# Block loads moved from the SP queue to GpSimd's queue with a cast, in a matmul with rotary embedding on one Trainium2 core

## Chip, core and metric

The kernel runs on one core of one Trainium2 chip. The metric is device time in microseconds (us) of a whole execution. A profile gives the span between the first and the last instruction; in the profiled runs the time is 1.8 us more than the span (161.65 and 159.9 before). The profiled run of before is not one of the four timed ones below. "Slow" is a run that takes over 1.5% more than the fastest of the same kernel in the same call, "fast" any other; the ratios use fast runs alone, while a median quoted is that of all runs unless said.

## The reference

```python
# x (16, 512, 768), weight (768, 768), cos and sin (512, 64), 12 heads of 64
y = np.matmul(x, weight).reshape(batch, seq, n_heads, head_dim)
y1, y2 = y[..., :32], y[..., 32:]
out1 = y1 * cos1 - y2 * sin1
out2 = y2 * cos2 + y1 * sin2
return np.concatenate([out1, out2], axis=-1).reshape(batch, seq, hidden)   # fp32
```

## The kernel before

The rows are worked through in 64 tiles of 128 rows, two tiles to a pair, 32 pairs. A tile has to be cast to FP16 and transposed before TensorE can multiply it. Most tiles ("plain") are cast by ScalarE, transposed by TensorE into PSUM and copied out by ScalarE. Every third pair from pair 8 on (8, 11, ... 29, "block pairs") spares TensorE the transposes: VectorE transposes 32 x 32 blocks. For that a block pair is loaded in four quarters, each to 32 partitions.

```python
BLOCKS = range(8, NP, 3)                 # NP = 32 pairs
xpool = ctx.enter_context(tc.tile_pool(name="xpool", bufs=8))    # plain tiles, fp32
bpool = ctx.enter_context(tc.tile_pool(name="bpool", bufs=3))    # block pairs, fp32
...
def load_quarter(n, q):
    ...
    src = x[b : b + 2].rearrange("b (j a r) (q k) -> r q a (b j) k", r=SB, a=R, q=NQ)
    dst = xbs[n].rearrange("p s (j k) -> p (s j) k", j=NQ)
    nc.sync.dma_start(out=dst[ts(q, R)], in_=src[r, q])     # 32 partitions, 256 rows of 768 bytes

def load_pair(n):
    if n >= NP or n in BLOCKS:
        return
    for s in (0, 1):
        load(n, s)                                          # 128 partitions, rows of 3072 bytes
        for m in (n + 1, n + 2):
            if m in BLOCKS:
                load_quarter(m, (0, 2, 1, 3)[2 * (n + 2 - m) + s])
...
def transpose_blocks(n, s):
    xT = tpool.tile([P, NT, P, 2], FP16, tag="xT", name="xT")
    nc.vector.transpose(out=xT.bitcast(FP32).rearrange("p t m e -> p (t m e)"),
                        in_=x16.pop((n, s)).bitcast(FP32))
...
def rope_pair(n, step=2 * H):
    ps = psys[n].rearrange("p b n -> p (b n)")
    for c in range(0, 2 * H, step):
        rope(n, c, c + step, ps[:, ds(c, step)])            # VectorE: PSUM times cos and sin
        add(n, c, c + step, nc.gpsimd)                      # GpSimd: the sum, into the output tile
...
for n in range(2, NP):
    load_pair(n + AHEAD - 2)                                # AHEAD = 7
    for s in (0, 1):
        for c in CHUNKS:
            mm(n, s, *c)
        upto("turn", 2 * n + s + 3)                         # transposes ahead
        upto("cast", 2 * n + s + 5)                         # casts ahead, ScalarE
    ...
    if n >= 3:
        store(n - 3, nc.scalar)
    rope_pair(n, H if n == NP - ALONE - 1 else 2 * H)       # ALONE = 4
```

## Time and profile before

| | before |
|---|---|
| time, four runs | 163.4, 163.8, 164.32 and (slow) 166.51 us; median 164.06, of the fast ones 163.8 |
| span of the profiled run | 159.9 us |
| TensorE / VectorE / ScalarE / GpSimd busy | 93 / 77 / 55 / 69% |
| bytes moved, mean rate | 53.13 MB, 332 GB/s |

### The profile page before, as it was taken

The numbers are of one execution on the slowest core, as the hardware profiler recorded it, in microseconds if no ns is written. First come the engines' busy times: TensorE is split into PE (matmuls) and PEld (weight loads), VectorE is DVE, ScalarE is ACT, GpSimd is POOL, SyncE is SP. The second block draws the span as 40 slices with busy tenths as digits, with TensorE's granted clock in tenths as the row PEclk, the third lists the DMA queues.
The fourth block names the chain that finished last, engine by engine and source line by source line (L and its number), as shares of the span: only waits on it lengthen the run. The fifth ranks groups of instructions, "written<-read, shape, count | busy, mean of one in ns | idle before, by whom it ended". The sixth has DMA issues, their size and how long they took to land.

```text
span 159.9 us, 2729 instructions
## 1 busy us (share of the span) xinstructions
PE 148.0 (93%) x1074; PEld 93.5 (58%) x1074; DVE 123.1 (77%) x77; ACT 87.6 (55%) x109; POOL 110.9 (69%) x43
## 2 busy tenths in 40 slices
PE   7999999999999999999999999299999999999920
PEld 2455666666666666666666666166667666665610
DVE  0566966788697697697889696459696898699990
ACT  3431966776827746674875854494956697200000
POOL 1000397777888878878878887735868778999990
PEclk9999999999999999999999999999999999999995
DMA  5999999999999999999999999999999999699655
GB/s 172 329 413 395 403 326 267 294 328 370 386 407 268 297 406 364 221 350 414 285 322 404 294 410 398 295 309 376 262 353 388 342 415 373 231 394 377 246 214 197
DMA packets 25837, 53.13 MB, mean 332 GB/s; under 512 B 2016, under 2 KB 10720, under 8 KB 25824
## 3 DMA queue, kind: packets, MB, share of 16 engines
q1 hardware_dynamic: 17056, 28.06, 57.2%
q10 hardware_dynamic: 8768, 24.91, 39.6%
q8 instruction: 8, 0.13, 0.3%
q14 instruction: 5, 0.04, 0.1%
HBM read 27.79 MB, written 25.17 MB: 331 GB/s over the span
## 4 chain that ended last, share of the span: by engine, by line
PE 65%; DMA 23%; DVE 5%; POOL 2%; ACT 2%; issue 1%; POOLq 0%; ACTq 0%; DVEq 0%
PE psy L169 52%; DMA xb<-in_x_dram 10%; PE pt L128 7%; DMA xs<-in_x_dram 7%; DMA out_dram<-ov 7%; DVE tq L183 3%; PE psy L253 3%; PE psz L169 2%; POOL ov L194 2%; ACT xT L72 1%; DVE xT L74 1%; ACT xc L72 1%; DVE xc L74 1%; POOLq L392 0%; ACTq L243 0%
## 5 line engine op out<-in xcount | busy, mean ns | idle before, releaser
L194 POOL TENSOR_TENSOR ov<-tq 128x1536 f32<-128x1536 f32 (+2 forms) x37 | 110.2, 2988 | 44.7 <-DVE tq L183 44.7
L169 PE MATMUL psy<-w_sb,xT 128*128 128x256 f16 (+1 forms) x733 | 126.5, 326 | 0.4 <-DVE w_sb L112 0.2
L183 DVE TENSOR_TENSOR tq<-psy,csn 128x3072 f32<-128x3072 f32 (+3 forms) x39 | 102.9, 2658 | 21.4 <-PE psy L169 20.0
L169 PEld LDWEIGHTS <-xT 128*128 128x128 f16 x769 | 73.4, 98 | 45.3 <-issue 0.6
L72 ACT COPY xT<-pt 128x768 f16<-128x768 f16 x46 | 36.4, 799 | 31.5 <-PE pt L128 31.5
L72 ACT CAST xc<-xs 128x768 f16<-128x768 f32 x46 | 40.8, 904 | 17.8 <-DMA xs<-in_x_dram 17.7
L128 PE MATMUL pt<-ident,xc 128*128 128x128 f16 x288 | 23.9, 221 | 3.4 <-ACT xT L72 3.1
L128 PEld LDWEIGHTS <-xc 128*128 128x128 f16 x288 | 20.0, 99 | 10.3 <-ACT xc L72 3.1
L72 ACT CAST xc<-xb 128x768 f16<-128x768 f32 x16 | 14.3, 903 | 0.5 <-issue 0.4
L135 DVE STREAM_TRANSPOSE xT<-xc 128x384 f32<-128x384 f32 x16 | 8.5, 557 | 3.2 <-ACT xc L72 3.2
L253 PE MATMUL psy<-cold 128*128 128x512 f16 x17 | 6.5, 528 | 1.2 <-DVE cold L260 1.2
L169 PE MATMUL psz<-w_sb,xT 128*128 128x512 f16 (+1 forms) x36 | 6.3, 326 | 0.0
L112 DVE CAST w_sb<-w_raw 128x768 f16<-128x768 f32 (+2 forms) x7 | 3.4, 501 | 2.0 <-DMA w_raw<-in_weight_dram 2.0
L183 DVE TENSOR_TENSOR tq<-psz,csn 128x512 f32<-128x512 f32 (+1 forms) x5 | 4.3, 897 | 0.1
L74 DVE CAST xc<-xs 128x768 f16<-128x768 f32 x2 | 1.9, 948 | 2.9 <-DMA xs<-in_x_dram 2.9
L253 PEld LDWEIGHTS <-cold 128*128 128x128 f16 x17 | 2.0, 128 | 3.5 <-issue 2.2
L74 DVE COPY xT<-pt 128x768 f16<-128x768 f16 x2 | 1.1, 558 | 1.9 <-PE pt L128 1.9
L72 ACT ACT_TABLE_LOAD x1 | 1.3, 1283 | 0.7 <-PEq L378 0.7
L260 DVE MEMSET cold<- 128x256 uint32 x1 | 0.3, 272 | 0.9 <-PEq L378 0.9
L226 DVE TENSOR_TENSOR ov<-psz,tq 128x512 f32<-128x512 f32 x1 | 0.7, 692 | 0.0
L222 DVE TENSOR_TENSOR psz<-psz,csn 128x512 f32<-128x512 f32 x1 | 0.7, 690 | 0.0
L222 DVE TENSOR_TENSOR tq<-psz,csn 128x512 f32<-128x512 f32 x1 | 0.7, 681 | 0.0
(8 smaller groups left out, 1.4 us busy)
## 6 DMA issues: line engine op xcount, KB each, us to landing
out_dram<-ov ACTq DMA_DIRECT2D x28, 768.0 KB, 8.0
xs<-in_x_dram SPq DMA_DIRECT2D x48, 384.0 KB, 8.1
xb<-in_x_dram SPq DMA_DIRECT2D x32, 192.0 KB, 8.7
out_dram<-ov ACTq DMA_DIRECT2D x7, 384.0 KB, 2.4
w_raw<-in_weight_dram SPq DMA_DIRECT2D x5, 384.0 KB, 6.9
w_raw<-in_weight_dram SPq DMA_DIRECT2D x1, 256.0 KB, 5.6
out_dram<-ov SPq DMA_DIRECT2D x1, 256.0 KB, 2.9
w_raw<-in_weight_dram SPq DMA_DIRECT2D x1, 128.0 KB, 5.5
```

The costliest lines, as they stand in the source:

```text
L72: eng.copy(out=o, in_=i_)
L74: eng.tensor_copy(out=o, in_=i_)
L112: nc.vector.tensor_copy(out=w_sb[:, t, e, c0:c1], in_=w_raw[:, t, e, c0:c1])
L128: nc.tensor.transpose(pt[:, t, e, :], xc[:, t, e, :], ident)
L135: nc.vector.transpose(out=xT.bitcast(FP32).rearrange("p t m e -> p (t m e)"), in_=x16.pop((n, s)).bitcast(FP32),)
L169: nc.tensor.matmul(ps[:, a - lo : z - lo], xTT[n, s][:, t, e, :], w_sb[:, t, e, a:z], start=((t, e) == CHUNKS[0] and n > 1), stop=((t, e) ...
L183: nc.vector.tensor_tensor(out=tqs[n][:, :, c0:c1].rearrange("p j (h d) -> p j h d", d=D), in0=ps.rearrange("p (h d) -> p h d", d=D) .unsqu ...
L194: eng.tensor_tensor(out=ovs[n][:, ds(c0, w)].rearrange("p (h t d) -> p h t d", t=2, d=HD), in0=tq[:, 0].rearrange("p (h t d) -> p h t d", ...
L222: nc.vector.tensor_tensor(out=o, in0=ph, op=MULT, in1=csn[:, j, n % SB, :].unsqueeze(1).broadcast_to((P, nh, D)),)
L226: nc.vector.tensor_tensor(out=ovs[n][:, c0:c1].rearrange("p (h t d) -> p h t d", t=2, d=HD), in0=ps.rearrange("p (h t d) -> p h t d", t=2, ...
L253: nc.tensor.matmul(psys[n][:, b], cold[:, 0:P], cold, start=True, stop=opened[0] < WARM - 6)
L260: nc.vector.memset(cold, 0.0)
```

## The change

The intent: GpSimd's DMA queue takes the quarter loads off the queue of the plain loads, casts them on the way, so that ScalarE has nothing to cast for them, and issues them early enough to be hidden. The core of the diff:

```diff
+    AHEAD_B = 8
-    xpool = ... bufs=8        bpool = ... bufs=3
+    xpool = ... bufs=10       bpool = ... bufs=5     # block pairs now FP16
...
-            nc.sync.dma_start(out=dst[ts(q, R)], in_=src[r, q])        # in load_quarter, fp32
+        for q in quarters:                                             # in load_blocks, FP16
+            nc.gpsimd.dma_start(out=dst[ts(q, R)], in_=src[r, q])
...
     def transpose_blocks(n, s):
-            out=xT.bitcast(FP32).rearrange("p t m e -> p (t m e)"),
-            in_=x16.pop((n, s)).bitcast(FP32),
+            out=xT.bitcast(FP32).rearrange("p t (j a) o -> p t j (a o)", j=NQ),
+            in_=x16.pop((n, s)).bitcast(FP32).rearrange("p (j a t) -> p t j a", j=NQ, t=NT),
...
-                cast(n, s, nc.scalar)
+                if n not in BLOCKS:
+                    cast(n, s, nc.scalar)
...
+    nc.gpsimd.tensor_copy(out=mark, in_=xss[3, 0][:, 0:1])   # waits for an early plain load
+    load_blocks(BLOCKS[0], (0, 2))
+    load_blocks(BLOCKS[0], (1, 3))
     rope_pair(0)
...
+        for m, quarters in ((n + AHEAD_B, (0, 2)), (n + AHEAD_B - 1, (1, 3))):
+            if m > BLOCKS[0]:
+                load_blocks(m, quarters)
...
-            rope_pair(n, H if n == NP - ALONE - 1 else 2 * H)
+            rope_pair(n, H if n >= NP - ALONE - 2 else 2 * H)
```

## The prediction

> **What bounds the kernel now.** I read the page's busy shares first, then the groups of instructions by shape, the waits, the timeline of one stall and of the end, and the DMA queues. Busy shares and queues:
>
> ```profile
> PE 148.0 (93%) x1074; PEld 93.5 (58%) x1074; DVE 123.1 (77%) x77; ACT 87.6 (55%) x109; POOL 110.9 (69%) x43
> ...
> q1 hardware_dynamic: 17056, 28.06, 57.2%
> q10 hardware_dynamic: 8768, 24.91, 39.6%
> ```
>
> TensorE is busy for 93% of the 159.9 us span. In the chain of waits its product of one tile comes again and again as 12 matmuls in 1.95 us and a transposed tile as 0.34 us, so it streams at one rate. Idle TensorE is found in three places only: 1.2 us at the start, one hole of 3.1 us, and 8.7 us at the end, where it has finished at 151.2. The two DMA queues' packets together take 96.8% of the 16 engines' time. So there are two near-bounds, TensorE and the transfers.
>
> The hole, in the timeline of before (start, length, engine, instruction, idle time before it and what ended that):
>
> ```profile
> 102.00 0.89 ACT L72 CAST xc<-xs 128x768 f16<-128x768 f32 x1 [2.68 <-DMA xs<-in_x_dram]
> ...
> 103.63 0.49 PE L128 MATMUL pt<-ident,xc 128*128 128x128 f16 x6 [3.14 <-ACT xT L72]
> ```
>
> ScalarE sat in a cast whose load had not landed; the copy that frees TensorE's transpose bank stood behind it. Load lateness is what makes this kernel lose TensorE time. In all, ScalarE waits for plain loads 17.7 us, most of it hidden. The instruction order shows why loads run late: all hardware DMAs share eight completion semaphores, so a load is issued only when the DMA eight places earlier has landed. In the waits of the queue that issues loads the largest mid-kernel entries are therefore stores, which nothing in the data asks for:
>
> ```profile
> SPq L93 <- DMA out_dram<-ov: 19.2, 4, 5.7
> SPq L79 <- DMA xs<-in_x_dram: 18.9, 15, 3.8
> ```
>
> GpSimd's row decides the case. The groups by shape, then three consecutive adds in the timeline:
>
> ```profile
> L194 POOL TENSOR_TENSOR ov<-tq 128x1536 f32<-128x1536 f32 x27 | 93.5, 3465 | 44.7 <-DVE tq L183 44.7
> L183 DVE TENSOR_TENSOR tq<-psy,csn 128x3072 f32<-128x3072 f32 x27 | 90.6, 3357 | 20.0 <-PE psy L169 18.6 <-PE pt L128 1.3
> ```
> ```profile
> 75.00 3.47 POOL L194 TENSOR_TENSOR ov<-tq 128x1536 f32<-128x1536 f32 x1 [0.77 <-DVE tq L183]
> ...
> 79.24 3.48 POOL L194 TENSOR_TENSOR ov<-tq 128x1536 f32<-128x1536 f32 x1 [0.77 <-DVE tq L183]
> ...
> 83.81 3.47 POOL L194 TENSOR_TENSOR ov<-tq 128x1536 f32<-128x1536 f32 x1 [1.09 <-DVE tq L183]
> ```
>
> Three pairs take 13.04 us (adds start at 57.73, 70.77, 83.81). GpSimd's three adds take 3 x 3.465 = 10.40, so 2.64 us are free (0.77 + 0.77 + 1.09 in the brackets). Of its 44.7 us of waiting 17.2 lie before the first add at 18.50. At the end it has none:
>
> ```profile
> 136.07 20.12 POOL L194 TENSOR_TENSOR ov<-tq 128x1536 f32<-128x1536 f32 x11 [0.81 <-DVE tq L183]
> ```
>
> From 136.07 to 156.2 it adds without a gap, then the last stores land. Whatever GpSimd is late by at 136 is added to the end.
>
> **What the Trainium skill says.** (1) "DMA: Bandwidth & Descriptors", section "SWDGE vs HWDGE vs iDMA": only a DMA issued by GpSimd can cast, and its descriptors are computed by software on GpSimd's cores; section "Latency and other measured facts" puts its first byte at about 1 us, the cores' emission overhead, against about 0.6 us from the other queues. Before has no such DMA, so no run here shows it yet. (2) "Perfetto Trace Analysis", section "DMA Instruction — SWDGE (GPSIMD)": cores 0 and 1 make the descriptors. These cores also add their own partitions, so I take descriptor time as lost to the adds. (3) "SBUF — State Buffer", section "Who interferes with whom": VectorE locks GpSimd out in 2-port modes, not in operations with one SBUF input. The ropes read PSUM and one SBUF operand, and GpSimd's adds hold 3.465 us beside them in before, so no lock shows there; I expect none.
>
> **The change, part by part.**
> *TensorE:* nothing. Both kernels use VectorE blocks for the same 8 pairs; the instruction counts are equal.
> *ScalarE:* loses the 16 casts of block tiles, 16 x 0.904 = 14.5 us, from 87.6 to about 73. It isn't the bound (55%); the gain is only fewer instructions in front of the copies.
> *VectorE:* the 16 block transposes (557 ns each) now read with a stride. I leave them at 0.56 and allow 0.15 us more, 2.4 us in all; its slack per three pairs is 13.04 - 3 x 3.357 - 1.03 = 1.94 us, so this hides. Pair 26 in halves adds 2 x 1.752 - 3.357 = 0.15 us.
> *Loads:* per three pairs the shared eight semaphores carry 4 plain loads and 3 stores, where they carried 4 more quarter loads: 7 instead of 11. A load then waits for a DMA issued 8/7 x 13.04 = 14.9 us earlier, not 9.5 us; plain buffers go from 8 to 10. The quarter loads have 8192 packets of 768 B. If the load queue's longer packets cost what the store queue's do (0.396 x 16 x 159.9 / 8768 = 116 ns), then of its 0.572 x 16 x 159.9 = 1463 us about 0.66 ms remain for them, some 80 ns each: 41 us of all 16 engines for 6.3 MB (an estimate). Writing half the bytes can only ease that. So I expect the hole of 3.1 us to go.
> *GpSimd:* gets 32 DMAs: 4 ahead of the first add (behind a small copy that waits for a load, at about 17.3 us by an estimate from ScalarE's casts at 15.3 and 17.8), and 28 in pairs 3 to 22, where the free time is 20 x 0.88 = 17.6 us. With c us per DMA, 28c - 17.6 is what it falls behind. Three rope buffers and two PSUM buffers let it lag about 6 to 7 us before TensorE stops: a rope three pairs on starts 3 x 4.35 - 3.36 = 9.7 us after the add's release, and the add takes 3.47 of that. In pairs 23 to 27 it regains some 4 us, then comes the gapless end. If it never idles, it needs 17.3 + 27 x 3.465 + 9 x 1.810 + 0.71 + 0.15 + 32c = 128.0 + 32c, and 3.7 us for the last store as now: **span = 131.7 + 32c**, unless TensorE's own floor of 159.9 - 3.1 = 156.8 is later. They cross at c = 0.78; the present span is met at c = 0.88.
>
> The profiled run took 161.65 us for a span of 159.9, so 1.75 us is added. The median of the timed runs is 164.32, 2.7 above that profiled run; I take that for more holes like the one shown (argued, not seen). Then c = 0.8 gives 159.1 us, 0.9 gives 162.3, 1.0 gives 165.5, 1.1 gives 168.7, 1.3 gives 175.1.
>
> **The rivals.**
> *A. GpSimd becomes the bound* (c about 1 or more). For: 2.64 us free against four DMAs per three pairs; each has 32 x 8 = 256 rows to describe on each side. That pair 26 is now halved too and the DMAs stop by pair 22 suggests a late GpSimd. Against: the skill speaks of a small incremental cost per descriptor. Time 164 to 175.
> *B. TensorE stays the bound and the load holes vanish* (c up to 0.8). For: the DMA share of 97%, the waits on stores. Against: it needs descriptors cheaper than the skill's first byte. Time 158.5 to 160.
> *C. The transfers become worse* through small casting packets on a third queue, so that plain loads are late still. For: they are near saturation now. Against: same packets, half the bytes written, more loads in flight. Time 163 to 168.
> *D. All is hidden*: holes removed, about as much lost to GpSimd. Time 161 to 166.
>
> **Range and chances.** The cost c decides. I take 1.0 from the skill as the likely value, which is 165.5 us; but the change looks balanced for GpSimd to catch up, and cheap descriptors leave a floor near 159, so I shade it to **163.5 us**, range **157.5 to 172**. Faster than 161.0 (2%) wants c below about 0.86: chance 0.34. Within 2%, c to about 1.06: 0.38. Slower than 167.6: 0.28.
>
> **What the new profile would show.** (1) ScalarE near 73 us with no casts of block tiles; block transposes at 0.55 to 0.7 us. (2) GpSimd's gaps between adds in pairs 3 to 22 growing by the issue time, and nothing left of its waits for VectorE if A holds; then VectorE waits for GpSimd, and TensorE for VectorE. Under B those waits stay positive and TensorE has no hole after 18.5 us. (3) Fewer waits of ScalarE for plain loads than 17.7 us, and the load queue waiting for buffers rather than for stores. (4) The end: the last add later than 156.2 under A, not under B. The prediction is wrong if an issue costs much under 0.8 us or over 1.3, if descriptor making runs beside the adds, or if casting packets are much slower than some 80 ns.

## More of the kernel before

The prediction shows the busy line, the groups and the waits. One more part of the page turned out to matter: the span in 40 slices of 4 us, with the busy share of the DMA engines in tenths and the rate.

```profile
DMA  5999999999999999999999999999999999699655
GB/s 172 329 413 395 403 326 267 294 328 370 386 407 268 297 406 364 221 350 414 285 322 404 294 410 398 295 309 376 262 353 388 342 415 373 231 394 377 246 214 197
```

The engines are busy nearly throughout, yet the rate swings between some 220 and 415 GB/s. The prediction read the first line and not the swing in the second.

## The result, and the profile after

The changed kernel took 158.42, 158.42, 158.49 and 158.75 us, median 158.45, against 164.06 before. The ratio is 0.966 (95% interval 0.960 to 0.971): the change is faster by 3.4%. Besides being lower, the times also agree better: within 0.4 us here and 0.5 us in the repeat, where the fast runs of before spread over 0.9 us here and 1.8 to 2.3 us later.

The busy line and the DMA queues of the changed kernel's page (queue, packets, MB, share of 16 engines' span):

```profile
PE 147.7 (94%) x1074; PEld 93.0 (59%) x1074; DVE 125.0 (80%) x78; ACT 74.6 (48%) x93; POOL 129.0 (82%) x77
...
q10 hardware_dynamic: 8768, 24.91, 41.0%
q1 hardware_dynamic: 8352, 21.76, 37.8%
q0 software_dynamic: 8704, 3.15, 17.2%
```

TensorE's work is the same; its span is shorter by the holes. In the changed kernel's waits TensorE waits 0.2 us for the second rope, at about 18.5 us, and for nothing after it. GpSimd went from 110.9 to 129.0 us. The groups of it that the change touches, by shape:

```profile
L192 POOL TENSOR_TENSOR ov<-tq 128x1536 f32<-128x1536 f32 x26 | 90.1, 3470 | 6.8 <-DVE tq L181 6.6
...
L103 POOL DMA_DIRECT2D xh<-in_x_dram x32 | 18.8, 591 | 0.0
L131 DVE STREAM_TRANSPOSE xT<-xh 128x384 f32<-128x384 f32 x16 | 10.6, 690 | 0.0
```

One issue costs GpSimd 0.59 us, not 1.0. The adds hold 3.47 us beside it, and what GpSimd waits for VectorE fell from 44.7 to 6.8 us (16.1 of the 17.2 us before the first add are now a wait of the small copy): it is nearly full, and no more. In the timeline of GpSimd three pairs look like this:

```profile
53.36 3.47 POOL L192 TENSOR_TENSOR ov<-tq 128x1536 f32<-128x1536 f32 x1 [0.47 <-DVE tq L181]
56.76 1.18 POOL L103 DMA_DIRECT2D xh<-in_x_dram  x2
57.94 3.49 POOL L192 TENSOR_TENSOR ov<-tq 128x1536 f32<-128x1536 f32 x1
61.34 1.16 POOL L103 DMA_DIRECT2D xh<-in_x_dram  x2
62.51 3.48 POOL L192 TENSOR_TENSOR ov<-tq 128x1536 f32<-128x1536 f32 x1
66.47 3.46 POOL L192 TENSOR_TENSOR ov<-tq 128x1536 f32<-128x1536 f32 x1 [0.48 <-DVE tq L181]
```

From 53.36 to 66.47 is 13.1 us, TensorE's own pace, with 0.48 us to spare. And the load queue (the longest wait of its own view) now waits for free buffers, that is for ScalarE's casts to empty them; loads run ahead of need:

```profile
SPq L81 <- ACT xc L74: 66.3, 29, 5.1
```

### The profile page after: what moved, and what is told of

Its sections match the earlier page's. It is cut to its first block, busy times and chain, and to the rows that moved or that the text cites. A ratio compares the mean times of both kernels' runs of the same rounds, so it can differ in the third digit from the quotient of the medians.

```text
span 156.6 us, 2722 instructions
## 1 busy us (share of the span) xinstructions
PE 147.7 (94%) x1074; PEld 93.0 (59%) x1074; DVE 125.0 (80%) x78; ACT 74.6 (48%) x93; POOL 129.0 (82%) x77
## 3 DMA queue, kind: packets, MB, share of 16 engines
q0 software_dynamic: 8704, 3.15, 17.2%
## 4 chain that ended last, share of the span: by engine, by line
PE 84%; DMA 5%; DVE 4%; SPq 2%; POOL 1%; POOLq 0%; issue 0%; DVEq 0%
PE psy L167 73%; PE pt L124 9%; DMA w_raw<-in_weight_dram 5%; DVE tq L181 3%; PE psz L167 2%; POOL ov L192 1%; SPq L108 1%; SPq L81 1%; POOLq L398 0%; DVE w_sb L111 0%; POOLq L192 0%; DVEq L181 0%
## 5 line engine op out<-in xcount | busy, mean ns | idle before, releaser
L124 PE MATMUL pt<-ident,xc 128*128 128x128 f16 x288 | 23.4, 219 | 0.6 <-DVE xc L76 0.6
L103 POOL DMA_DIRECT2D xh<-in_x_dram x32 | 18.8, 591 | 0.0
L328 POOL COPY mark<-xs 128x1 f32<-128x1 f32 x1 | 0.2, 183 | 16.1 <-DMA xs<-in_x_dram 16.1
L131 DVE STREAM_TRANSPOSE xT<-xh 128x384 f32<-128x384 f32 x16 | 10.6, 690 | 0.0
```

The lines of the kernel that those rows point to most:

```text
L103: nc.gpsimd.dma_start(out=dst[ts(q, R)], in_=src[r, q])
L124: nc.tensor.transpose(pt[:, t, e, :], xc[:, t, e, :], ident)
L131: nc.vector.transpose(out=xT.bitcast(FP32).rearrange("p t (j a) o -> p t j (a o)", j=NQ), in_=x16.pop((n, s)).bitcast(FP32).rearrange("p ( ...
```

## The experiments

Four theories of why the loads of before are late were put up, and two questions about GpSimd. DEPTH: too few buffers. BYTES: the quarter loads move too many bytes. PACKETS: their rows of 768 bytes are too short. ORDER: 32 more DMAs stand in the load queue and occupy the eight semaphores that all hardware DMAs share, so that a load is issued only when the DMA eight places earlier has landed. A fifth, WIDTH (the quarters go to only 32 partitions), came out of the runs. There were three calls, each on another chip (7, 14 and 12 on record). Each ran the kernel before as well; its median was 162.43, 163.05 and 162.56 us, so a kernel that keeps the whole gain shows a ratio of about 0.975 here (the changed kernel's repeat: 0.975), not the 0.966 of the first comparison. Where an interval reaches over 0.980 (no cast, small loads, one wide load, pair 26 whole) the kernel is surely faster than before, but not surely by 2%.

**Depth alone, on the kernel before.**

```diff
-    xpool bufs=8, bpool bufs=3
+    xpool bufs=10, bpool bufs=5
```

> The kernel before with the changed kernel's buffer counts only (plain tiles 8 to 10, block tiles 3 to 5). If the depth of the buffers is what mends late loads (theory DEPTH), it lands near the changed kernel's 158.5 us, at most 160. If loads are late because quarter loads and stores hold the eight shared DMA semaphores and the load queue stands in order behind them (theory ORDER), or because the quarter loads' bytes cost too much transfer time (theory BYTES), it stays within 1.5 us of the kernel before, 162.5 to 165, and the load queue still waits some 30 us in all for stores.

Measured: 162.84 us, ratio to before 0.9985 (0.990 to 1.007): the same (one of the four runs was slow; the fast ones have 162.82). DEPTH falls.

**The changed kernel without the cast.** The quarters stay FP32, GpSimd issues them at the same places, ScalarE casts them, VectorE transposes them as before.

```diff
-            xhs[n] = bpool.tile([P, 2, H], FP16, ...)
+            xhs[n] = bpool.tile([P, 2, H], FP32, ...)
...
-                if n not in BLOCKS:
-                    cast(n, s, nc.scalar)
+                cast(n, s, nc.scalar)
```

> The changed kernel with FP32 quarters: GpSimd still issues them eight pairs ahead, but without a cast; ScalarE casts the 16 block tiles again and VectorE transposes them as before. Theory BYTES (the halved writes relieve the transfers) expects most of the gain lost: 161.5 to 164 us. Theory ORDER expects the gain kept: 158.3 to 159.5 us, with ScalarE back at about 88 us busy and block transposes back at 557 ns. The issue on GpSimd should still cost about 0.59 us if it is set by the number of rows, not by the cast.

Measured: 158.56 us, ratio 0.976, ScalarE at 87.1 us. The gain stays (interval 0.971 to 0.982). So the cast, the halved bytes and the 16 casts taken off ScalarE are together worth at most what that interval leaves open, some 0.5%: BYTES falls. Its issue's row among the groups by shape:

```profile
L103 POOL DMA_DIRECT2D xh<-in_x_dram x32 | 18.7, 589 | 0.0
```

The same 0.59 us, though this queue moved 2048 packets, four rows or more to a packet of data, where the casting one had 8704.

**The changed kernel with the buffers of before.**

```diff
-    xpool bufs=10, bpool bufs=5
+    xpool bufs=8, bpool bufs=3
```

> The changed kernel with the buffer counts of before (plain 8, blocks 3). Theory DEPTH expects the gain lost, 162 us or more. ORDER and BYTES expect at most 1 us lost: 158.4 to 159.5 us, with TensorE waiting for nothing after 18.5 us but the load queue waiting longer for ScalarE's casts than the 66 us of the changed kernel.

Measured: 158.25 us, ratio 0.974. The deeper buffers show no gain in either kernel.

**Small loads in the quarter loads' places.** To try ORDER without bytes, 32 loads of 1 KB were put into the changed kernel's SP queue.

```diff
                 load(n, s)
+                for m in (n + 1, n + 2):
+                    if m in BLOCKS:
+                        nc.sync.dma_start(out=scrap[:, small[0]], in_=x[0, 0:16, 0:16])
+                        small[0] += 1
```

> The changed kernel with 32 loads of 1 KB added on the plain loads' queue, in the places the quarter loads had in the kernel before; they carry no weight (32 KB in all) but take their turn in the eight shared semaphores and the queue's order. ORDER expects much of the loss back: 160.5 to 164 us, with waits for stores in the load queue of 15 us or more and late casts on ScalarE. BYTES and DEPTH expect no change: 158.3 to 159.2 us.

Measured: 158.68 us (158.26 to 159.98), ratio 0.978. Of the load queue's waits in this run:

```profile
SPq L93 <- DMA out_dram<-ov: 16.7, 8, 3.0
```

The waits for stores are back, as ORDER says, and they cost almost nothing. A miss for ORDER as it stood: the number of DMAs in the queue isn't what hurts when they are small. (Small loads land soon, so the run says nothing of large ones.) (The 159.98 run is the profiled one; it had a TensorE hole of 1.5 us where VectorE waited 3.1 us for a block load.)

**Long rows, on the kernel before.** The quarter loads keep number, bytes, partitions and place, but fetch 64 rows of 3072 bytes for 256 of 768. The block pairs' data are wrong on purpose, and so was the result.

```diff
-        src = x[b : b + 2].rearrange("b (j a r) (q k) -> r q a (b j) k", r=SB, a=R, q=NQ)
-        dst = xbs[n].rearrange("p s (j k) -> p (s j) k", j=NQ)
-        nc.sync.dma_start(out=dst[ts(q, R)], in_=src[r, q])
+        src = x[b : b + 2].rearrange("b (a c r) h -> r c a b h", r=SB, a=R)
+        nc.sync.dma_start(out=xbs[n][ts(q, R)], in_=src[r, q])
```

> The kernel before, whose quarter loads keep their number, bytes, partitions, queue and place but fetch 64 rows of 3072 bytes where they fetched 256 of 768 (so the block pairs get the wrong data, on purpose: the result will be wrong, the dependences and the work are the same). Theory PACKETS (short packets on the hardware queue take the engines' time and so make all later loads late): most of the gain, 158.3 to 160 us, and the load queue's share of the engines falls from 57% to about 38 to 46%. Theory ORDER (32 more DMAs in the queue's order and in the eight shared semaphores are what hurts): stays at 161.5 to 164 us with waits for stores of some 30 us in the load queue.

Measured: 161.51 us (one of the four runs was slow; the fast ones have 161.3), ratio 0.992 (0.985 to 0.999). PACKETS accounts for about a third of the gain (0.8%, where the change's repeat gained 2.5%), and the interval allows from almost nothing to 1.5%. The load queue's share fell only to 54.9%, not to the 38 to 46% that PACKETS said, and the time is about what ORDER said. This run's only profile is of its slow run (163.35 us).

**One wide load for a block pair, on the kernel before.** The same bytes and long rows once more, in one DMA to all 128 partitions; wrong data.

```diff
+        if q == 0:
+            src = x[b : b + 2].rearrange("b (p r) h -> r p b h", r=SB)
+            nc.sync.dma_start(out=xbs[n], in_=src[r])
```

> The kernel before, whose four quarter loads of a block pair are one load of the same bytes (768 KB, 128 partitions, long rows, in the place of the first quarter; wrong data for the block pairs, on purpose). Per three pairs the eight shared semaphores then carry 8 DMAs, not 11. Sharpened theory ORDER (the number of DMAs in flight is capped at eight, so with 11 per 13.04 us each may take only 8 x 13.04 / 11 = 9.5 us from issue to landing, and they take 8.0 to 8.7 in the median and up to 11): now 13.0 us are allowed and the gain of the change appears without GpSimd, 158.3 to 159.8 us. If only the short packets and bytes mattered it equals the run with long-row quarter loads, 161.5 us.

Measured: 158.74 us, ratio 0.977 (0.973 to 0.981). The gain of the change appears with no GpSimd DMA, no cast, and ScalarE at 87 us.

This is what the sharpened ORDER had forecast, and the run changes the number of the loads as well as their width, so its time doesn't tell ORDER from WIDTH. What speaks for WIDTH is the table of stretches of 2 us in one and the same phase of the four kernels (stretch, its length, busy time of the five engines with counts, TensorE clock, busy share of the DMA engines, GB/s). Before:

```profile
46.00:48.00 2.00, 2.00 (x19) 1.37 (x17) 2.00 (x1) 0.30 (x1) 2.00 (x1) 1.00 1.01 405
48.00:50.00 2.00, 2.00 (x17) 1.25 (x16) 1.12 (x2) 1.32 (x3) 1.23 (x2) 1.00 1.07 327
50.00:52.00 2.00, 2.00 (x17) 1.34 (x16) 2.00 (x1) 1.59 (x2) 2.00 (x1) 1.00 1.06 210
52.00:54.00 2.00, 2.00 (x17) 1.25 (x15) 1.08 (x1) 1.58 (x2) 1.23 (x2) 1.00 1.07 262
```

With long rows, still to 32 partitions (the slow run):

```profile
50.00:52.00 2.00, 2.00 (x17) 1.23 (x15) 2.00 (x1) 1.60 (x2) 2.00 (x1) 1.00 1.02 238
52.00:54.00 2.00, 2.00 (x19) 1.34 (x18) 1.26 (x1) 1.55 (x2) 1.22 (x2) 1.00 1.03 263
```

With one wide load:

```profile
50.00:52.00 2.00, 2.00 (x17) 1.24 (x15) 1.98 (x1) 1.61 (x2) 2.00 (x1) 1.00 1.04 417
52.00:54.00 2.00, 2.00 (x19) 1.34 (x18) 1.38 (x1) 1.43 (x2) 1.24 (x2) 1.00 1.02 402
```

With FP32 quarters of 32 partitions, but on GpSimd's queue (by the packet records they are moved here from 47 to 50.5 and from 52 to 55 us, so hardly at all in the second line):

```profile
48.00:50.00 2.00, 2.00 (x18) 1.28 (x16) 1.12 (x2) 1.32 (x2) 1.99 (x4) 1.00 1.03 361
50.00:52.00 2.00, 2.00 (x17) 1.32 (x16) 2.00 (x1) 1.60 (x2) 2.00 (x1) 1.00 1.03 404
52.00:54.00 2.00, 2.00 (x17) 1.27 (x15) 1.10 (x1) 1.58 (x2) 1.57 (x2) 1.00 1.04 375
```

The load queue of before issued three quarter loads and three plain loads between 44.9 and 48.3; when these come to be moved, the rate falls to about half. From 50 to 54 us no packet of a store is moved in before; a third of the bytes are the quarters' and two thirds the plain loads'. The lack of stores isn't the reason: with one wide load, 0.78 of the 0.83 MB from 50 to 52 us are loads too, at 417 GB/s. The engines' share (packet times added up, so it can pass 1) stays above 1 meanwhile. If a cap on the number of DMAs in flight were the limit, I would expect idle engines; these are busy and slow. Of the 50 stretches of 2 us from 20 to 120 us, 13 are at a share of 0.99 or more and yet under 280 GB/s in before, 11 with long rows, 1 with one wide load, 2 with FP32 quarters on GpSimd's queue. The packet records agree: in before 22% of the plain loads' packets of 3072 bytes take over 180 ns (219 ns in the median of those), with one wide load 2%, in the changed kernel 2%, with FP32 quarters on GpSimd's queue 6%; the ordinary packet takes 121 to 124 ns. With long rows it is 24% of the load queue's, but there the quarters' own packets are of this size and can't be told apart. Over 20 to 120 us the mean rate is 336 GB/s in before, 345 with long rows, 376 with one wide load and 375 with FP32 quarters on GpSimd's queue.

The trace of the run with FP32 quarters has one stretch that ORDER can't explain. Its first four quarters, issued together at 17.4 us, are moved from 21 to 27 us beside plain loads alone:

```profile
20.00:22.00 2.00, 2.00 (x18) 1.41 (x17) 1.70 (x1) 1.22 (x3) 2.00 (x1) 1.00 1.05 386
22.00:24.00 2.00, 2.00 (x18) 1.29 (x16) 1.07 (x1) 1.30 (x3) 2.00 (x2) 1.00 1.00 242
24.00:26.00 2.00, 2.00 (x19) 1.34 (x18) 2.00 (x1) 1.31 (x3) 2.00 (x1) 1.00 1.08 277
```

They stand in neither the hardware queue nor its eight semaphores, and yet the rate falls, and the plain packets take 175 to 205 ns in the mean of each us from 22 to 27.

So the theory that fits best is WIDTH: FP32 loads to 32 partitions that are moved beside plain loads bring the rate of both down to about half. This is read from the traces; no run changed the width alone. Nor is every dip of this kind: the one under one wide load (261 GB/s from 72 to 74 us) lies in stores' packets of 229 ns. The Trainium skill, "SBUF — State Buffer", section "Door 1: The DMA port swizzle", says that 32 partitions reach 8 of the 16 DMA ports, for at most about 218 GB/s. No run here shows a narrow load by itself; the slow stretches of before, plain loads included, move 202 to 276 GB/s (202 at 64 to 66 us), against about 415 beside them, which fits.

**Plain loads in four, on the changed kernel.** The converse.

```diff
-        nc.sync.dma_start(out=xss[n, s], in_=src)
+        for q in range(NQ):                                    # for pairs from AHEAD on
+            nc.sync.dma_start(out=xss[n, s][ts(q, R)], in_=src[ts(q, R)])
```

> The changed kernel with every plain load after the first fourteen cut in four of 32 partitions: same bytes, same packets of 3072 bytes, block loads still by GpSimd, but 19 hardware DMAs per three pairs on the eight semaphores, which allows 8 x 13.04 / 19 = 5.5 us from issue to landing. ORDER expects late casts again, 161 us or more, and the queue waiting for other DMAs instead of for buffers. If only bytes and packets mattered, nothing changes: 158.3 to 159.2 us.

Measured: 168.9 and 171.0 us in its two fast runs (slow: 171.45 and 173.38). In the waits ScalarE's for plain loads, 8.2 us in the changed kernel, has grown:

```profile
ACT xc L74 <- DMA xs<-in_x_dram: 41.9, 23, 4.7
```

The mean rate from 20 to 120 us is 293 GB/s at a share of 1.05: again busy and slow. But ORDER had forecast this too (161 us or more), and the load queue does wait for other DMAs again, 29.0 us for stores alone. Number and width both changed, so this run doesn't tell them apart; I read it as WIDTH for the busy share alone.

**The price of an issue.** Each of the 32 GpSimd DMAs cut into two of 128 rows.

```diff
-            nc.gpsimd.dma_start(out=dst[ts(q, R)], in_=src[r, q])
+            for h in (0, 4):
+                nc.gpsimd.dma_start(out=dst[ts(q, R), h : h + 4], in_=src[r, q][:, h : h + 4])
```

> The changed kernel with each of GpSimd's 32 DMAs cut in two of 128 rows (64 DMAs, the same bytes). If an issue's 0.59 us is a fixed price, 64 of them take 38 us; by the prediction's sum the span is 131.7 + 38 = 169 us and the time about 171 us, with GpSimd waiting for nothing and TensorE waiting for ropes. If the price goes by rows, an issue takes about 0.30 us, GpSimd's total stays near 19 us and the time near 158.5 us.

Measured: 169.31 us, ratio 1.042, span 167.5. The issue's row among the groups by shape, then, from the waits, VectorE's for GpSimd to free a rope buffer:

```profile
L104 POOL DMA_DIRECT2D xh<-in_x_dram x64 | 34.7, 550 | 0.0
```
```profile
DVE tq L184 <- POOL ov L195: 11.6, 9, 2.2
```

Half the rows cost 0.55 us instead of 0.59. The price is nearly fixed, and 64 of them make GpSimd the bound.

**The dear case of the prediction, made.** One add of 256 elements behind each DMA.

```diff
             nc.gpsimd.dma_start(out=dst[ts(q, R)], in_=src[r, q])
+            nc.gpsimd.tensor_tensor(out=busy, in0=csn[:, 0], in1=csn[:, 1], op=ADD)
```

> The changed kernel with one extra add of 256 elements (about 0.71 us) behind each of GpSimd's 32 DMAs, so that a DMA costs GpSimd 0.59 + 0.71 = 1.30 us, the dear case of the prediction. Its sum says span 131.7 + 32 x 1.30 = 173.3 us, time about 175 us, GpSimd without waits from 17.4 us to the end. If GpSimd's lag is hidden by buffers after all, the time is nearer 160 us.

Measured: 173.09 us, ratio 1.066, span 171.3. The added work among the groups by shape, and from the waits again the one on GpSimd:

```profile
L105 POOL TENSOR_TENSOR busy<-csn 128x256 f32<-128x256 f32 x32 | 23.7, 742 | 0.4
```
```profile
DVE tq L185 <- POOL ov L196: 20.6, 11, 2.6
```

GpSimd's lag isn't hidden. The prediction's sum with the measured durations gives 131.7 + 32 x (0.602 + 0.742) = 174.7 us of span, 2% over the measured one. Busy times overlap: in the timeline after, an add of 3.47 us is followed 3.40 us after its start.

**Pair 26 whole again, on the changed kernel.**

```diff
-            rope_pair(n, H if n >= NP - ALONE - 2 else 2 * H)
+            rope_pair(n, H if n == NP - ALONE - 1 else 2 * H)
```

> The changed kernel with pair 26 roped and added whole, as before. All theories of the loads expect 158.3 to 158.8 us; the halves' purpose is to let GpSimd start earlier at the gapless end, so undoing it may cost up to 0.7 us (half an add less half a rope) if GpSimd is what ends the kernel, and nothing if the last TensorE product is.

Measured: 158.84 us, ratio 0.977 (0.972 to 0.982); the changed kernel's repeat below has 0.975. What the halves bring, 0.4 us at most by the medians, stays inconclusive.

**A try at a better version: a ninth block pair.**

```diff
-    BLOCKS = range(8, NP, 3)
+    BLOCKS = range(5, NP, 3)      # quarters of pairs 5 and 8 issued before pair 2
```

> A try at a better version: pair 5 becomes a ninth block pair (its quarters and those of pair 8 are issued before pair 2). TensorE loses 12 transposes, 0.67 us; GpSimd gets four more issues of 0.59 us early, where the load of the first tiles is on too, and has 6.8 us of waits to pay them with. Expected 157.7 to 158.3 us; if the first pairs' loads come late by the added short packets, 159 or more.

**The changed kernel again, as the yardstick.** No edit.

> The changed kernel once more, on the chip of this call, as the yardstick for the ninth block pair and the other two: 158.2 to 158.9 us.

Measured: 161.58 us (ratio 0.995) for the ninth block pair and 158.48 us (0.975) for the changed kernel. The timeline of the run with the ninth shows why:

```profile
33.66 1.29 DVE L131 STREAM_TRANSPOSE xT<-xh 128x384 f32<-128x384 f32 x2 [2.38 <-DMA xh<-in_x_dram]
```

The quarters issued from 17.8 to 20.2 us had landed only at 33.6; by the packet records they were moved beside plain loads, about one packet of 384 bytes for each of 3072. TensorE stood 2.4 us, and the next tile's 12 matmuls took 3.35 us where they take 2.1. In the changed kernel a block load takes 9.6 us to land in the median and 16.6 at most: that is what eight pairs of lead, some 35 us, are for. No version run here beats the changed kernel; the one with fewer buffers, 158.25 us, equals it with less memory.

## Why the prediction was right or wrong

**Right in range and, by the lesser part of its chances, in direction.** 158.45 us lies inside 157.5 to 172. The point, 163.5, was 5.1 us too high, and "faster" had only 0.34.

**The step that failed: the cost c of an issue on GpSimd**, "I take 1.0 from the skill as the likely value". It measured 0.59 us, which the prediction itself had named as a sign of being wrong ("much under 0.8 us"). The skill's figure is the time to the first byte; it isn't the time for which GpSimd is held. With 0.59 the prediction's own sum gives 131.7 + 32 x 0.59 = 150.6 us, below TensorE's floor, so rival B holds: its floor of 156.8 us of span stands against 156.6 measured, its 158.5 to 160 us against 158.45.

**The sum itself was right.** The two runs that loaded GpSimd more landed within 2% of it (131.7 + 64 x 0.55 = 166.9 us against 167.5 for the cut DMAs, 174.7 against 171.3 for the added work), so GpSimd does become the bound when a quarter load costs it 1.1 or 1.34 us. The margin is thin: 2.64 us free against 4 x 0.59 = 2.36 in three pairs.

**Right on the holes.** That load lateness costs TensorE its time, and that the timed runs of before have more such holes than the profiled one, fits what came: the holes went, and the spread of the times with them. ScalarE at 74.6 us (about 73 was said), block transposes at 690 ns (0.55 to 0.7), the load queue waiting for buffers, the last add ending before 156.2 (at 152.8 in the timeline): all as said for B. One reading of before was off: TensorE's last products end at 153.0 us, not 151.2, so it stands 6.9 us at the end and not 8.7; the floor of 156.8 us doesn't use it.

**Wrong on the cause of lateness.** The prediction named the eight shared semaphores, since the queue's waits read so. Those waits are there, but a wait for a semaphore says only that an earlier DMA hasn't landed, not why. The runs show that the quarter loads in the plain loads' queue are what hurts, and not buffers, the cast or a mere count of small DMAs; the traces point to the width of these loads, which slow the plain loads even outside that queue (242 GB/s), and the rate line of the page had shown the slow stretches before the change. That the holes would go was thus right partly by luck: taking the quarters off the queue mends lateness under either cause.

**Wrong on the short packets.** The estimate gave them 80 ns each and 41 us in all. Their records show 45 ns in the mean, 8192 x 45.4 / 16 = 23 us; most of the rest was in the plain packets, slow beside them (153 ns in the mean, against 121 in the median). "Writing half the bytes can only ease that" was no gain at all: the casting packets took 51.6 ns in the mean, 26 us in all, more than the 23 us before.

**What stays open.** From GpSimd's queue the FP32 quarters slow the plain loads from 22 to 27 us, and hardly from 32 to 72 us (34 of 1911 plain packets over 180 ns). Why wasn't separated: the issue in pairs of quarters 0 with 2 and 1 with 3, their spreading in time and the stores between came together there. No run changed width and kept the number of DMAs; that part rests on the busy shares and packet times, and whether ORDER adds something for large loads no run tells.

## What to carry to other kernels

Where the DMA engines are busy but their rate swings, look for the narrow loads in the queue before looking at bytes, buffers or semaphores: here the rate of the queue fell to half while a few loads to 32 partitions stood in it (plain packets of 219 ns instead of 121). A swing has other causes too, so try the narrow loads made wide before you rebuild. GpSimd's queue was a way round them at a nearly fixed price per DMA (0.55 us for 128 rows, 0.59 for 256), so count issues, not rows, against GpSimd's free time per period, and give such loads several periods of lead. A wait for a DMA's semaphore names what was waited for, not the cause.

## What the Trainium skill lacked or had wrong

- "DMA: Bandwidth & Descriptors", section "Latency and other measured facts", gives about 1 us to the first byte and calls it the emission overhead; it has no figure for how long an issue holds GpSimd. Here 0.59 us for 256 rows with a cast, 0.59 without, 0.55 for 128 rows.
- The same page, section "SWDGE vs HWDGE vs iDMA", gives a packet as preferably at most 4096 bytes. The FP32 quarters from GpSimd went in 512 packets of 3072 and 1024 of 4608 bytes by the packet records; the casting ones in 8192 packets of 384 bytes, so by these records its rows were not joined.
- "SBUF — State Buffer", section "Door 1: The DMA port swizzle", has the rate of a narrow DMA by itself, but not what goes with it for wide ones in its queue: 22% of their 3072-byte packets over 180 ns, 219 in the median instead of 121, and 2.3% of the kernel's time between before and the run with one wide load (which has fewer loads too).
